# Modulation products in float32r parts, gate products ranked behind the main stream, one modulation vector moved

## The chip, the cores and the metric

The kernel runs on one core of a Trainium2 chip. The metric is device time in microseconds (us) for one launch, the median of several runs. TensorE (PE) multiplies; VectorE (DVE), ScalarE (ACT) and GpSimd (POOL) work on tiles; SyncE (SP) issues the DMA transfers.

## The reference

One inference step of a two-layer diffusion backbone for 128 context and 512 latent tokens, all in float32, outputs included. In each layer:

```python
sh1, sc1, g1, sh2, sc2, g2 = split(silu(c) @ w_mod + b_mod, 6)      # "modulation vectors" 0..5
h = rmsnorm(x, g_pre_mix) * (1 + sc1) + sh1
qa, ka, va, qbd, kvbd, kbr, qc, kc, vc, gates = split(h @ w_in)
oa, ob, oc = mixer A (windowed), mixer B (multi-head latent), mixer C (rotary)   # attention, 8 heads each
m = sum over A, B, C of sigmoid(gate) * (o @ w_o);  mixed = m @ w_out
x = x + g1 * rmsnorm(mixed, g_post_mix)
h = rmsnorm(x, g_pre_mlp) * (1 + sc2) + sh2
x = x + g2 * rmsnorm(square(relu(h @ w_mlp1)) @ w_mlp2, g_post_mlp)
```

The modulation uses one conditioning vector for the latent tokens and another for the context tokens.

## The kernel before

Tokens are five tiles of 128, features eight chunks of 128. A float32 product is made of three float32r products: each operand is split into a high part (ACT copies it to float32r: `wh`, `hh`) and a low part (DVE subtracts: `wl`, `hl`), and `mm3` adds high x high, high x low and low x high in PSUM. Weights come as 128x1024 pieces (`unit`): one DMA into `wr`, then the two splits.

The start (`first_norm`): the five token tiles `x` are normalised and transposed (`xn`, `nps`, `hf`). In the meantime modulation vectors 1 and 0 of layer 0 are computed, in two halves of 512 columns: eight transfers of 1 MB (`mw`) bring the weights, and plain float32 matmuls (`lps<-mw,scT`, 32 of them, 2x512 out) multiply them with the two conditioning vectors `scT`. A row of sums (`modrow`) is copied out by ACT, transposed (`modt`) and added to the bias (`modT`, `gsT`); with these `hf` is scaled and shifted and split into `hh` and `hl`. Then mixer B's projection begins: 288 columns (`sps<-wh,hh`, its weights split ahead of the second half's modulation), in a first round over chunks 0 to 3 of all five token tiles and a second over chunks 4 to 7, and then 384 columns.

The gates (`gate_gen`, L1573): 24 pieces of 128 columns per layer, each in two halves of 24 matmuls (`gps`), a tanh (`th`) and a store. They are the work with which other stages are filled: `drive` steps through a main generator and adds credit at a rate to the streams beside it; at credit 1 a stream records one step (one gate half, or one `w_mod` piece). In mixer B the gates' rate is `GATE_RATE_B` for seven heads and 1 in the last; in A and C it is `GATE_RATE`; what is left at the end of C is recorded at once, and four halves go into the merge. The other filler is `mod_gen`: the remaining modulation vectors, on DVE (`macc`: 14 of 16 steps are a multiply-add on 128x512), ten steps per vector. Before the change each layer computes vectors 2, 3, 4 beside A and C, and layer 0's MLP computes vector 5 and layer 1's 0 and 1.

What is recorded is then put in order by a planner (`Recorder.schedule`): a list scheduler with a cost for each operation (`cost`) chooses for each engine, at the time that it models, the ready operation of the lowest rank. On TensorE the rank is the place in the record, less `high_priority`'s offset; on the others it is the latest time from the pass before. The instructions are emitted in that order, all from one line, L528, and each engine works through its own in order. In mixer B the PSUM banks are two pairs (`big`) and a ring of four, shared by `tps` (transposed probabilities), `ops` (their products with the values), `pjps`, `qrps` and `gps`.

Of the kernel before, what the change touches and what calls it, by code (L numbers as in the profile page):

```python
# [11 lines left out]
F32 = mybir.dt.float32  # L12
# [5 lines left out]
P = 128  # L18
D = 1024
KC = 8  # L20
# [11 lines left out]

GATE_RATE = ((0.3, 0.3, 0.235, 0.241), (0.213, 0.3, 0.195, 0.156))
PROJ_RATE = ((0.26, 0.583, 0.277), (0.326, 0.93, 0.22))
GATE_RATE_B = 0.03
MOD_RATE = 0.3
MOD_RATE_B = 0.0
GATES_LAST = 4
GATES_FIRST = 2
LAG = 2  # L40
# [7 lines left out]
KEPT = 4  # L48
ACT_BUFS = 10
UP_RATE = (0.5, 0.5)  # L50
DOWN_RATE = (1.0, 0.5)

# [115 lines left out]
class Recorder:  # L168
# [23 lines left out]
    def cost(self, op, outs, ins):  # L192

        n = outs[0].idx.size if outs else 1
        e, name = op.eng, op.name
        if op.dma:
            return 0.4, 0.4
        if e == "tensor":
            passes = 4 if name == "matmul" and ins[-1].dt == F32 else 1
            t = max(0.108, n * passes / 2400 + 0.013)  # L200
            return t, t + 0.17
        src = max([v.idx.size for v in ins] or [n])
        if e == "vector":
            if name == "scalar_tensor_tensor":
                t = 0.21 + 1.04e-3 * src
            elif name in ("tensor_scalar", "tensor_copy"):
                t = 0.16 + (1.04e-3 if any(v.root.space == "PSUM" for v in ins) else 0.54e-3) * src
            else:
                t = 0.15 + 1.04e-3 * src
            return t - 0.08, t  # L210
        if e == "scalar":
            t = 0.19 + 0.83e-3 * src
            if any(isinstance(op.kw.get(k), View) for k in ("bias", "scale")):
                t += 0.09
            if "accum_out" in op.kw:
                t += 0.1
            return t - 0.1, t
        if name == "tensor_scalar":
            t = 0.3 + 0.8e-3 * src
        elif op.kw.get("op") == ALU.pow or ALU.pow in op.args:  # L220
            t = 0.4 + 0.16 * src
        else:
            t = 0.15 + 2.25e-3 * src
        return t, t


    def record(self, eng, name, args, kw):
# [12 lines left out]
            v = op.views[0]  # L240
            op.wait = (v.hi - v.lo) * v.idx.size * 4
        op.time = op.busy, op.wait
        op.both = eng == "gpsimd" and name == "tensor_tensor" and outs[0].idx.size > 4
        for views, write in ((ins, False), (outs, True)):
            for v in views:
                r, m, keep, seen = v.root, v.mask(), [], False
# [139 lines left out]
    def one(self, everything, look):  # L386
# [3 lines left out]
        now = {e: [] for e in engines}  # L390
        order, self.done, self.given = [], [], []
        count = 0
        pool_end, net, half = 0.0, 0.0, 0.0

        def less(s, t, todo):
            nonlocal count
# [39 lines left out]
        while True:  # L436
# [32 lines left out]
            if o.dma:  # L469
                net = max(net, t + 1.6) + wait / 370e3  # L470
                wait = net + 0.7 - t
            elif e == "vector" and o.sb and pool_end > t:
                more = 0.62 * min(pool_end - t, busy / 0.38)
                busy, wait = busy + more, wait + more
            elif o.both:
                busy, wait = 1.2 * busy, 1.2 * wait
                pool_end = t + busy
            elif e == "tensor":
                if t - free[e] > 2.6:
                    half = t + (6.8 if t - free[e] > 4 else 3.4)  # L480
                if t < half:
                    busy, wait = 2 * busy, wait + busy
# [49 lines left out]
class Step:  # L532
# [70 lines left out]
    def setup(self, ctx):  # L603
# [34 lines left out]
        self.gkc = c.tile([P, 64], F32, name="gkc")  # L638
        self.sink = c.tile([P, 8], F32, name="sink")
        self.scT = c.tile([P, 2, 8], F32, name="scT")  # L640
        self.modT = [c.tile([P, 6, 8, 2], F32, name=f"modT{l}") for l in range(DEPTH)]
        self.vecT = [c.tile([P, 64], F32, name=f"vecT{l}") for l in range(DEPTH)]
        self.gsT = [c.tile([P, 2, 8, 2], F32, name=f"gsT{l}") for l in range(DEPTH)]
# [21 lines left out]
    def cond(self):  # L665

        nc, I = self.nc, self.I
        cT = self.sm.tile([P, 16], F32, name="cT")
        self.small_rows_T(cT, [I["c"].rearrange("o (a b) -> (o a) b", b=P), I["c_ctx"].rearrange("(a b) -> a b", b=P)])
        e = self.sm.tile([P, 16], F32, name="ce")  # L670
        nc.scalar.activation(e, cT, AF.Exp, scale=-1.0)
        nc.vector.tensor_scalar(e, e, 1.0, None, ALU.add)
        r = self.sm.tile([P, 16], F32, name="cr")
        nc.vector.reciprocal(r, e)
        nc.vector.tensor_tensor(self.scT.rearrange("p s k -> p (s k)"), cT, r, ALU.mult)
        for l in range(DEPTH):
# [146 lines left out]
    def first_norm(self, pool, xin):  # L823
# [17 lines left out]
        mod, gs = self.modT[0], self.gsT[0]  # L841
        w = I["w_mod"][0]
        for n in range(2):
            if n == 1:
                self.first = self.proj_units(I["w_in"][0], 768 + 384, 288, 3)
            for v in (1, 0):
                ps = self.lin_ps()
                for kh in range(2):
                    raw = pool.tile([P, 4, 512], F32, name="mw", tag="mw", bufs=8)
                    nc.sync.dma_start(raw, self.wsrc(w, 4 * kh, 4, v * D + n * 512, 512))  # L850
                    for i in range(4):
                        k = 4 * kh + i
                        nc.tensor.matmul(ps[:2, :], self.scT[:, :, k], raw[:, i], start=k == 0, stop=k == KC - 1)
                row = pool.tile([2, 512], F32, name="modrow", tag="modrow", bufs=2)
                nc.scalar.activation(row, ps[:2, :], AF.Copy)
                tps = self.bank("modt", "pt")
                pv = tps[:, :8].rearrange("p (n s) -> p n s", s=2)
                for j in range(4):
                    nc.tensor.transpose(pv[:, j, :], row[:, j * P:j * P + P], self.ident[:2, :2])
                ks = slice(4 * n, 4 * n + 4)  # L860
                nc.vector.tensor_tensor(mod[:, v, ks], pv, self.vecT[0][:, 8 * v:8 * v + 8][:, ks].unsqueeze(2).to_broadcast([P, 4, 2]), ALU.add)
                if v:
                    self.gains(0, 0, ks)
            for k in range(4 * n, 4 * n + 4):
# [5 lines left out]
                        nc.vector.tensor_scalar(hf[:, k, c], hf[:, k, c], g, b, ALU.mult, ALU.add)  # L870
                nc.scalar.activation(self.hh[:, k, :], hf[:, k, :], AF.Copy)
                nc.vector.tensor_tensor(self.hl[:, k, :], hf[:, k, :], self.hh[:, k, :].bitcast(F32), ALU.subtract)


    def proj_units(self, w, c0, n, kn):
# [700 lines left out]
    def gate_gen(self, pool, l):  # L1576
# [3 lines left out]
        for n in range(24):  # L1580
            wh, wl = self.unit(self.wsrc(w, 0, 8, 2208 + n * P, P), (8, P))
            for hf in range(2):
                c = slice(hf * NH, hf * NH + NH)
                ps = self.bank("gps", self.gtag)
                for k in range(KC):
                    self.mm3(ps[:, :NH], wh[:, k, :], wl[:, k, :], self.hh[:, k, c], self.hl[:, k, c], k == 0, k == KC - 1)
                th = pool.tile([P, NH], F32, name="th", tag="th", bufs=2)
                nc.scalar.activation(th, ps[:, :NH], AF.Tanh, scale=0.5)
                nc.sync.dma_start(self.th_d[l][n][:, c], th)
# [323 lines left out]
    def run(self):  # L1913
        nc, tc, I, O = self.nc, self.tc, self.I, self.O
        with ExitStack() as ctx:
# [23 lines left out]
            for l in range(DEPTH):  # L1939
                self.fine = False  # L1940
                stack2 = ExitStack()
                fpool = stack2.enter_context(pool(f"fill{l}", sides[1 - l % 2]))
                mods = [self.mod_gen(fpool, l, (2, 3, 4))]
                gates_left = self.gate_gen(fpool, l)
                gl = [itertools.islice(gates_left, 48 - GATES_LAST)]
                fills = gl + mods
# [98 lines left out]
                with pool(f"up{l}", side) as mp:  # L2045
# [4 lines left out]
                    modp = fstack.enter_context(pool(f"md{l}", hside))  # L2050
                    mods = [self.mod_gen(modp, l, (5,), 2)]
                    if not last:
                        mods = [itertools.chain(*mods, self.mod_gen(modp, l + 1, (0, 1), 2))]
                    kept = {"pool": kstack.enter_context(pool(f"kept{l}", hside))}
                    halfs = self.halfs()

# [99 lines left out]
```

## Time and profile before

| | us |
|---|---|
| median of 3 runs (2334.31 to 2335.96) | 2334.68 |
| the profiled execution | 2327.95 |
| its span, first to last instruction | 2326.2 |
| PE busy | 2277.6 |
| DVE busy | 1705.0 |
| ACT busy | 1204.0 |

The profile comes from one execution, which took less than the median of the runs shown. A matmul's busy time reaches past the point at which the next can start, so idle time of PE is larger than the listed one.

### The profile page before, as it was taken

What the parts mean: (1) busy time and instruction counts of PE and PEld (TensorE: products, weight loads), DVE (VectorE), ACT (ScalarE), POOL (GpSimd) and SP (SyncE); (2) the same over time, 40 slices, a digit from 0 to 9 for tenths busy, and PEclk for the clock granted to TensorE, in tenths of its full rate; (3) what the DMA queues carried; (4) which work ended last, traced back from release to release, by engine and by line L of the source; (5) the groups of instructions that cost most, each with busy time, mean ns of one, the idle gap of its engine ahead of it and who ended that gap; (6) DMA issues with size and microseconds to landing.
All of it is one profiled execution on the core that took longest, in us unless ns stands there. A gap on an engine that the chain in (4) does not pass through costs nothing. (4 is left out here: it accounts for less than half of the span.)

```text
span 2326.2 us, 39127 instructions
## 1 busy us (share of the span) xinstructions
PE 2277.6 (98%) x14303; PEld 2086.7 (90%) x14303; DVE 1705.0 (73%) x3707; ACT 1204.0 (52%) x2860; POOL 260.8 (11%) x315
## 2 busy tenths in 40 slices
PE   8999999999999999999999999999999999999998
PEld 4988999999998999888889889999899999998886
DVE  3688598997675998767377867999947569895445
ACT  5477455566435555632265764656643356554222
POOL 1023022222001000000021211222210000000000
PEclk9999999999999999999999999999999999999999
DMA  7431334333663454755244222434346545536332
GB/s 258 117 84 53 88 111 137 106 109 97 225 207 113 151 184 144 241 190 165 68 136 116 65 79 80 138 101 123 110 145 205 172 136 177 166 127 208 121 118 82
DMA packets 252448, 317.08 MB, mean 136 GB/s; under 512 B 37328, under 2 KB 169696, under 8 KB 251744
## 3 DMA queue, kind: packets, MB, share of 16 engines
q1 hardware_dynamic: 252256, 314.58, 43.6%
q8 instruction: 113, 1.85, 0.3%
q14 instruction: 79, 0.65, 0.1%
HBM read 251.84 MB, written 57.44 MB: 133 GB/s over the span
## 5 line engine op out<-in xcount | busy, mean ns | idle before, releaser
L528 ACT ACTIVATE wh<-wr 128x256 fp32r<-128x256 f32 (+5 forms) x772 | 273.7, 420 | 306.2 <-PE lps L528 166.5
L528 DVE TENSOR_TENSOR wl<-wr,wh 128x256 fp32r<-128x256 f32 (+5 forms) x772 | 303.4, 441 | 147.9 <-ACT wh L528 143.0
L528 PE MATMUL lps<-wh,ah 128*128 128x512 f32 x640 | 253.0, 395 | 0.0
L528 PE MATMUL lps<-wh,al 128*128 128x512 f32 x640 | 252.4, 394 | 0.0
L528 PE MATMUL lps<-wl,ah 128*128 128x512 f32 x640 | 251.6, 393 | 0.0
L528 POOL TENSOR_SCALAR pt<-pt,rc 128x640 f32<-128x640 f32 (+1 forms) x192 | 174.1, 915 | 629.4 <-DVE rc L528 523.2
L528 POOL TENSOR_TENSOR rs<-ss,mhalf 128x1 f32<-128x1 f32 x60 | 39.1, 652 | 1302.7 <-DVE ss L528 1302.7
L528 DVE TENSOR_TENSOR pl<-tps,ph 128x512 fp32r<-128x512 f32 (+2 forms) x240 | 147.9, 630 | 31.1 <-ACT ph L528 28.4
L528 ACT ACTIVATE pt<-sps,nm 128x640 f32<-128x640 f32 (+2 forms) x192 | 141.7, 741 | 42.1 <-DVE nm L528 36.3
L528 ACT ACTIVATE ph<-tps 128x512 fp32r<-128x512 f32 (+2 forms) x240 | 130.2, 556 | 35.4 <-PE tps L528 33.1
L528 PEld LDWEIGHTS lps<-wl,ah 128*128 128x128 f32 x640 | 120.1, 188 | 28.6 <-issue 0.5
L528 PEld LDWEIGHTS lps<-wh,ah 128*128 128x128 f32 x640 | 120.2, 188 | 27.8 <-issue 0.5
L528 PEld LDWEIGHTS lps<-wh,al 128*128 128x128 f32 x640 | 120.1, 188 | 27.6
L528 PE MATMUL sps<-h2h,wh 128*128 128x320 f32 (+2 forms) x464 | 144.3, 311 | 0.0
L528 PE MATMUL tps<-ident,pt 128*128 128x128 f32 x896 | 140.5, 275 | 3.6 <-POOL pt L528 2.9
L528 PE MATMUL sps<-h2l,wh 128*128 128x320 f32 (+2 forms) x464 | 143.1, 308 | 0.0
L528 PE MATMUL sps<-h2h,wl 128*128 128x320 f32 (+2 forms) x464 | 143.1, 308 | 0.0
L528 DVE SCALAR_TENSOR_TENSOR macc<-wr,scT,macc 128x512 f32<-128x512 f32 x168 | 126.4, 786 | 6.0 <-DMA wr<-in_w_mod 5.7
L528 PE MATMUL gps<-hh,wh 128*128 128x320 f32 x384 | 120.0, 312 | 2.7 <-ACT th L528 1.8
L528 PE MATMUL gps<-h2h,wh 128*128 128x320 f32 x384 | 119.7, 312 | 0.2 <-DVE pl L528 0.2
L528 PEld LDWEIGHTS tps<-ident,pt 128*128 128x128 f32 x896 | 106.7, 141 | 14.5 <-POOL pt L528 5.5
L528 PE MATMUL sps<-ol,wh 128*128 128x320 f32 x384 | 118.6, 309 | 0.5 <-DVE ol L528 0.5
(329 smaller groups left out, 6785.2 us busy)
## 6 DMA issues: line engine op xcount, KB each, us to landing
wr<-in_w_in SPq DMA_DIRECT2D x72, 512.0 KB, 4.0
wr<-in_w_mlp SPq DMA_DIRECT2D x72, 512.0 KB, 4.0
wq<-in_w_mlp SPq DMA_DIRECT2D x56, 512.0 KB, 4.0
wr<-in_w_mod SPq DMA_DIRECT2D x48, 512.0 KB, 3.8
ar<-a SPq DMA_DIRECT2D x56, 320.0 KB, 3.8
mr<-in_w_mod SPq DMA_DIRECT2D x32, 512.0 KB, 5.9
th<-th SPq DMA_DIRECT2D x96, 160.0 KB, 2.0
tg<-th SPq DMA_DIRECT2D x48, 320.0 KB, 3.5
```

The lines of the kernel that those rows point to most:

```text
L528: getattr(getattr(self.nc, o.eng), o.name)(*args, **kw)
```

## The change

The 32 float32 products of the start become 64 float32r ones: ACT and DVE split each 128x512 block of `w_mod` into `wh` and `wl`, the conditioning vectors are split once (`scs`: two high columns, two low ones), and each block is multiplied with all four columns, so that the row of sums has four rows, added in pairs behind the transposes. The split of mixer B's first weights is recorded behind both halves instead of between them. Gate matmuls are recorded with an offset of 200 places to the rear, and the gates' rate beside mixer B is 0.1 in place of 0.03. Vector 2 of layer 1 is computed in layer 0's MLP, in place of beside layer 1's mixers. The planner's costs of some operations are changed.

```diff
-GATE_RATE_B = 0.03
+GATE_RATE_B = 0.1
+GATES_BEHIND = 200
-DOWN_RATE = (1.0, 0.5)
+DOWN_RATE = (1.3, 0.5)
...
         if e == "tensor":
-            passes = 4 if name == "matmul" and ins[-1].dt == F32 else 1
-            t = max(0.108, n * passes / 2400 + 0.013)
+            if ins[-1].dt == F32:
+                t = n * 4 / 2400 + 0.013 if name == "matmul" else 0.108
+                t = max(0.18, t) if name == "matmul" else t
+            else:
+                t = n / 2400 + (0.018 if n > 400 else 0.013) if n > 128 else 0.085
...
             if "accum_out" in op.kw:
-                t += 0.1
+                return t, t
...
-        op.both = eng == "gpsimd" and name == "tensor_tensor" and outs[0].idx.size > 4
+        op.both = eng == "gpsimd" and name in ("tensor_tensor", "tensor_scalar") and outs[0].idx.size > 4
...
-                more = 0.62 * min(pool_end - t, busy / 0.38)
+                more = pool_hold * min(pool_end - t, busy / (1 - pool_hold))
...
+        for i in range(2):
+            nc.vector.tensor_copy(self.scs[:, :, i], self.scT[:, i, :])
+            nc.vector.tensor_tensor(self.scs[:, :, 2 + i], self.scT[:, i, :], self.scs[:, :, i].bitcast(F32), ALU.subtract)
...
-            if n == 1:
-                self.first = self.proj_units(I["w_in"][0], 768 + 384, 288, 3)
...
-                        nc.tensor.matmul(ps[:2, :], self.scT[:, :, k], raw[:, i], start=k == 0, stop=k == KC - 1)
...
+                        nc.scalar.activation(wh, raw[:, i], AF.Copy)
+                        nc.vector.tensor_tensor(wl, raw[:, i], wh.bitcast(F32), ALU.subtract)
+                        nc.tensor.matmul(ps[:4, :], self.scs[:, k, :], wh, start=k == 0, stop=False)
+                        nc.tensor.matmul(ps[:4, :], self.scs[:, k, :], wl, start=False, stop=k == KC - 1)
...
+                nc.vector.tensor_tensor(mod[:, v, ks], pv[:, :, 2:4], mod[:, v, ks], ALU.add)
...
+        self.first = self.proj_units(I["w_in"][0], 768 + 384, 288, 3)
...
-                for k in range(KC):
-                    self.mm3(ps[:, :NH], wh[:, k, :], wl[:, k, :], self.hh[:, k, c], self.hl[:, k, c], k == 0, k == KC - 1)
+                with self.tc.high_priority(offset=-GATES_BEHIND):
+                    for k in range(KC):
+                        self.mm3(ps[:, :NH], wh[:, k, :], wl[:, k, :], self.hh[:, k, c], self.hl[:, k, c], k == 0, k == KC - 1)
...
-                mods = [self.mod_gen(fpool, l, (2, 3, 4))]
+                mods = [self.mod_gen(fpool, l, (2, 3, 4) if l == 0 else (3, 4))]
...
-                        mods = [itertools.chain(*mods, self.mod_gen(modp, l + 1, (0, 1), 2))]
+                        mods = [itertools.chain(*mods, self.mod_gen(modp, l + 1, (0, 1, 2), 2))]
```

ScalarE at the start, before: the fifth token tile's normalisation to the first chunk scaled with the first half's modulation (`x_126` is the context tile, `hf_168` the transposed tokens, `modrow` the row of sums).

```order
L528 ACTIVATE xn,ss<-x_126 128x1024
L528 ACTIVATE hf_168<-nps 128x4x128 x2
L528 ACTIVATE modrow<-lps 2x512
L528 ACTIVATE hf_168<-nps 128x4x128 x2
L528 ACTIVATE modrow<-lps 2x512
L528 ACTIVATE hf_168<-hf_168,modT_281,gsT_283 128x512
L528 ACTIVATE hh<-hf_168 128x640
```

The same stretch of ScalarE now, from the first row of sums on (`wh<-mw` is the high part of a block of `w_mod`, `wh<-wr` that of mixer B's first weights).

```order
L533 ACTIVATE modrow<-lps 4x512
L533 ACTIVATE wh<-mw 128x512 x8
L533 ACTIVATE hf_173<-nps 128x4x128
L533 ACTIVATE modrow<-lps 4x512
L533 ACTIVATE wh<-mw 128x512 x9
L533 ACTIVATE modrow<-lps 4x512
L533 ACTIVATE wh<-mw 128x512 x4
L533 ACTIVATE wh<-wr 128x432
L533 ACTIVATE hf_173<-hf_173,modT_375,gsT_384 128x512
L533 ACTIVATE hf_173<-hf_173,modT_375,gsT_384 128x128
L533 ACTIVATE hh<-hf_173 128x640 x2
```

All 32 blocks of `w_mod` are split ahead of the first scaled chunk, and mixer B's first weights behind them; VectorE has its 32 `wl<-mw` in the same places.

TensorE in mixer B of layer 0, second pair of heads, before: the last scores and transposes ahead of the keys' projection (`sps<-ckh,wh`), which takes its PSUM pair over from `qd`, the queries.

```order
L528 MATMUL sps<-krT,qrT 128x320
L528 MATMUL tps<-ident,pt 128x128 x4
L528 MATMUL qrps<-identr,qrst 128x128 x4
L528 MATMUL ops<-ph,Vb 128x512
L528 MATMUL sps<-ckh,wh 128x384
L528 MATMUL sps<-ckl,wh 128x384
L528 MATMUL sps<-ckh,wl 128x384
```

The same place now (`gps` are gate products).

```order
L533 MATMUL sps<-krT,qrT 128x320
L533 MATMUL tps<-ident,pt 128x128
L533 MATMUL gps<-hl,wh 128x320
L533 MATMUL tps<-ident,pt 128x128
L533 MATMUL gps<-hh,wl 128x320
L533 MATMUL tps<-ident,pt 128x128
L533 MATMUL gps<-hh,wh 128x320
L533 MATMUL tps<-ident,pt 128x128
L533 MATMUL gps<-hl,wh 128x320
L533 MATMUL gps<-hh,wl 128x320
L533 MATMUL gps<-hh,wh 128x320
L533 MATMUL gps<-hl,wh 128x320
L533 MATMUL sps<-ckh,wh 128x384
```

Seven gate products now stand between the last scores and the keys' projection, one or a few at a time. Counted in TensorE's order from the first query product of mixer B (`sps<-qlh`) to the first key transposed for A (`kps`), gate products rise from 212 to 380 in layer 0 and from 216 to 384 in layer 1. From there to the last product of C's values they fall from 720 to 552 and from 580 to 552. Between the end of C and the first product of the merge, where nothing else is left, they fall from 48 to 34 in layer 0 and from 188 to 34 in layer 1. Places where TensorE changes between a gate product and another rise from 204 to 1132.

## Rows read from the trace of the kernel before

**Rows 1.** The page's first lines: span, and busy time of each engine.
```profile
span 2326.2 us, 39127 instructions
PE 2277.6 (98%) x14303; PEld 2086.7 (90%) x14303; DVE 1705.0 (73%) x3707; ACT 1204.0 (52%) x2860; POOL 260.8 (11%) x315
```

**Rows 2.** Busy time by stretch: bounds, length, engines (x instructions), granted clock, DMA.
```profile
core 0: us, PE busy (x) PEld busy (x) DVE busy (x) ACT busy (x) POOL busy (x), PEclk, DMA share, GB/s
0.00:45.20 45.20, 37.36 (x119) 12.04 (x119) 14.35 (x48) 22.41 (x41) 9.04 (x16) 1.00 0.89 308
112.00:225.00 113.00, 107.83 (x724) 97.85 (x722) 91.47 (x191) 84.09 (x195) 28.74 (x38) 1.00 0.27 70
225.00:259.00 34.00, 33.32 (x232) 32.52 (x232) 13.45 (x35) 13.82 (x39) 1.74 (x3) 1.00 0.36 110
...
950.00:1181.00 231.00, 231.00 (x1044) 189.54 (x1043) 146.30 (x279) 82.66 (x195) 6.94 (x9) 1.00 0.52 168
1254.00:1366.00 112.00, 107.03 (x718) 97.48 (x717) 93.73 (x194) 84.32 (x196) 28.22 (x37) 1.00 0.30 78
1430.00:1712.00 282.00, 274.94 (x1972) 258.34 (x1971) 255.91 (x624) 173.81 (x451) 71.84 (x79) 1.00 0.38 110
```

**Rows 3.** The same view for gate products alone (tile gps), mixer B, layer 0.
```profile
112.00:225.00 113.00, 7.34 (x47) 6.63 (x45) 0.87 (x2) 1.00 0.27 70
225.00:259.00 34.00, 25.98 (x168) 25.05 (x168) 3.07 (x7) 1.00 0.36 110
```

**Rows 4.** TensorE in order of time, mixer B: start, us, matmul.
```profile
138.84 0.50 PE L528 MATMUL ops<-ph,Vb 128*128 128x512 f32 x1
140.02 0.41 PE L528 MATMUL sps<-ckh,wh 128*128 128x384 f32 x1 [0.68 <-DVE qd L528]
```

**Rows 5.** Groups of 0 to 62 us: busy, mean ns, idle before.
```profile
L528 PE MATMUL lps<-mw,scT 128*2 128x512 f32 x64 | 29.1, 601 | 0.0
...
L528 DVE TENSOR_TENSOR hl<-hf,hh 128x640 fp32r<-128x640 f32 x8 | 6.2, 822 | 2.4 <-ACT hh L528 2.3
...
L528 ACT ACTIVATE hh<-hf 128x640 fp32r<-128x640 f32 x8 | 5.4, 723 | 0.0
...
L528 ACT ACTIVATE hf<-hf,modT,gsT 128x512 f32<-128x512 f32 x4 | 3.1, 808 | 2.8 <-DVE modT L528 2.8
```

**Rows 6.** TensorE in order of time: mixer B's first products of 288 and 384 columns.
```profile
45.23 0.40 PE L528 MATMUL sps<-wh,hh 128*128 128x288 f32 x1
...
63.12 0.39 PE L528 MATMUL lps<-wh,hh 128*128 128x384 f32 x1
```

**Rows 7.** VectorE in order of time: the low parts of chunks 4 to 7.
```profile
49.95 3.03 DVE L528 TENSOR_TENSOR hl<-hf,hh 128x640 fp32r<-128x640 f32 x4 [1.44 <-ACT hh L528]
```

**Rows 8.** DMA rate in 40 equal slices of 0 to 45.2 us.
```profile
GB/s 0 29 297 421 243 3 60 359 406 433 417 390 388 401 393 392 384 392 384 384 391 386 382 393 384 386 386 390 384 380 391 390 240 148 40 75 283 117 360 253
```

**Rows 9.** Groups of the whole span, shapes apart: busy, mean ns, idle before.
```profile
L528 DVE TENSOR_TENSOR pl<-tps,ph 128x512 fp32r<-128x512 f32 x176 | 118.0, 685 | 29.0 <-ACT ph L528 26.5
...
L528 DVE SCALAR_TENSOR_TENSOR macc<-mr,scT,macc 128x512 f32<-128x512 f32 x112 | 78.6, 744 | 5.3 <-DMA mr<-in_w_mod 5.0 <-ACT macc L528 0.2
...
L528 DVE TENSOR_TENSOR wl<-wr,wh 128x512 fp32r<-128x512 f32 x28 | 18.8, 682 | 3.0 <-ACT wh L528 2.7
...
L528 ACT ACTIVATE wh<-wr 128x512 fp32r<-128x512 f32 x28 | 16.1, 627 | 9.3 <-DMA wr<-in_w_in 9.1
```

**Rows 10.** TensorE in order of time: transposes of the first and the third token tile.
```profile
7.75 3.83 PE L528 MATMUL nps<-ident,xn 128*128 128x128 f32 x16
...
15.70 1.09 PE L528 MATMUL nps<-ident,xn 128*128 128x128 f32 x8 [0.94 <-POOL xn L528]
```

**Rows 11.** Busy time by stretch for tile macc alone, layer 1's A and C.
```profile
1430.00:1712.00 282.00, 11.22 (x72) 8.92 (x72) 61.56 (x83) 3.60 (x5) 1.00 0.38 110
```

More of the change, by code (lines that the diff above doesn't have):

```diff
@@ L392, in one @@
         count = 0
-        pool_end, net, half = 0.0, 0.0, 0.0
+        pool_end, pool_hold, net, half = 0.0, 0.0, 0.0, 0.0
         def less(s, t, todo):
@@ L477, in one @@
                 pool_end = t + busy
+                pool_hold = 0.62 if o.name == "tensor_tensor" else 0.3
             elif e == "tensor":
@@ L640, in setup @@
         self.scT = c.tile([P, 2, 8], F32, name="scT")
+        self.scs = c.tile([P, 8, 4], F32R, name="scs")
         self.modT = [c.tile([P, 6, 8, 2], F32, name=f"modT{l}") for l in range(DEPTH)]
@@ L852, in first_norm @@
                         k = 4 * kh + i
-                        nc.tensor.matmul(ps[:2, :], self.scT[:, :, k], raw[:, i], start=k == 0, stop=k == KC - 1)
-                row = pool.tile([2, 512], F32, name="modrow", tag="modrow", bufs=2)
-                nc.scalar.activation(row, ps[:2, :], AF.Copy)
+                        if i % 2 == 0:
+                            hi = self.ws.tile([P, 1024], F32R, name="wh", tag="wh", bufs=self.NW)
+                            lw = self.ws.tile([P, 1024], F32R, name="wl", tag="wl", bufs=self.NW)
+                        wh, wl = (t[:, i % 2 * 512:i % 2 * 512 + 512] for t in (hi, lw))
+                        nc.scalar.activation(wh, raw[:, i], AF.Copy)
+                        nc.vector.tensor_tensor(wl, raw[:, i], wh.bitcast(F32), ALU.subtract)
+                        nc.tensor.matmul(ps[:4, :], self.scs[:, k, :], wh, start=k == 0, stop=False)
+                        nc.tensor.matmul(ps[:4, :], self.scs[:, k, :], wl, start=False, stop=k == KC - 1)
+                row = pool.tile([4, 512], F32, name="modrow", tag="modrow", bufs=2)
+                nc.scalar.activation(row, ps[:4, :], AF.Copy)
                 tps = self.bank("modt", "pt")
-                pv = tps[:, :8].rearrange("p (n s) -> p n s", s=2)
+                pv = tps[:, :16].rearrange("p (n s) -> p n s", s=4)
                 for j in range(4):
-                    nc.tensor.transpose(pv[:, j, :], row[:, j * P:j * P + P], self.ident[:2, :2])
+                    nc.tensor.transpose(pv[:, j, :], row[:, j * P:j * P + P], self.ident[:4, :4])
                 ks = slice(4 * n, 4 * n + 4)
-                nc.vector.tensor_tensor(mod[:, v, ks], pv, self.vecT[0][:, 8 * v:8 * v + 8][:, ks].unsqueeze(2).to_broadcast([P, 4, 2]), ALU.add)
+                nc.vector.tensor_tensor(mod[:, v, ks], pv[:, :, 0:2], self.vecT[0][:, 8 * v:8 * v + 8][:, ks].unsqueeze(2).to_broadcast([P, 4, 2]), ALU.add)
+                nc.vector.tensor_tensor(mod[:, v, ks], pv[:, :, 2:4], mod[:, v, ks], ALU.add)
                 if v:
```

## The prediction

> **What bounds the kernel now.** I read the page first: PE is busy 2277.6 of 2326.2 us [rows 1], so anything that doesn't shorten PE's own work, or its waits, moves nothing. Then the busy time by stretch. The reader is to see two kinds of stretch there. In the MLP PE is busy 231.00 of 231.00 us [rows 2]; nothing can be won but work. In mixer B's first seven heads it is idle 113.00 - 107.83 = 5.2 us in layer 0 and 112.00 - 107.03 = 5.0 in layer 1, in A and C of layer 1 282.00 - 274.94 = 7.1 [rows 2]. The listed idle time is too small: in the timeline a product begins at 138.84 and the next at 140.02, 1.18 us apart, and only 0.68 of it counts as idle, since a matmul's busy time runs past the point where the next could start [rows 4]. Adding, over the 724 matmuls of mixer B's stretch, what each start-to-start distance has above the usual one of its form gives some 13 us (an estimate), the same in layer 1, and 22 in layer 1's A and C. Gate products could stand in these holes, but the view for gate products shows 47 of them in the 113 us of seven heads, and 168 in the 34 us of the last [rows 3], where PE idles only 0.7 us [rows 2].
>
> **The change, part by part.**
>
> *The start.* PE loses 64 records (two for each of 32 products) that fill 29.1 us [rows 5] and gets 64 float32r products of the same columns; at half a record's time each pair costs what one record did, so about 14.5 us go. That is not the gain, since they stood in front of mixer B's first product at 45.23 [rows 6] without a pause, and the new ones wait for ACT and DVE. What ends last now? The transfers run at 380 to 400 GB/s until about 36 us [rows 8]; behind the last `w_mod` block come mixer B's first weights, 128 x 8 x 288 x 4 bytes = 1.18 MB, 3 us, so `w_mod` is there at about 33. Its last four blocks cost one ACT split (0.63) and four DVE splits (0.68 each) [rows 9]: 36.4, or 37 with the small instructions in between. One megabyte takes 2.7 us to come and 4 x 0.68 = 2.7 on DVE, so DVE just keeps pace. Mixer B's first product can start at about 38, 7 us earlier. But all scaling is now queued behind the splits on ACT: 8 `hh` (5.4), 4 wide scalings (3.1) [rows 5] and 13 smaller ones (four narrow scalings, a row of sums, eight weight halves) of at most 0.63: 14 to 17 us behind 35.6, so the last `hh` is done at 50 to 52 and its `hl` at 51 to 53. Before it was done at 49.95 + 3.03 = 52.98 [rows 7]. So the last chunk comes hardly earlier; what PE gains is that from 38 to 52 it works off the first round and most of the second. The stage of 288 columns took 63.12 - 45.23 = 17.9 us [rows 6]. Only chunk 7's products, 15 of 120, must wait for the end: 52 + 2 us plus transposes, 55 to 56, against 63.12. I take 6 us of these 7 or 8, since the fourth piece of the 384-column weights now waits for a `wr` buffer that is split late. Bounds: 8 us (17.9 us without a pause from 37.3), and nothing (PE works tile by tile, so that each tile waits for chunk 7, 52.98 + 10).
>
> *More gates beside mixer B.* The order puts 168 more gate matmuls there in each layer. The work is the same in sum; what counts is which holes it fills. They are taken from A and C (168 fewer in layer 0, 28 in layer 1) and from the lump behind C in layer 1, which falls from 188 to 34: there PE has nothing to fill. Where the keys' projection waited for `qd` (0.68 listed), seven gate products now stand ahead of it. Three such waits, the scores' and the transposes' are the bulk of the 13 us. From both ends: all of it filled, 13 us per layer; nothing filled, since the planner's times are not the chip's and a hole is often not where a gate stands, 0; less than nothing is the slower rival below. I take a third, 4.5 us per layer, 9 in both: nearer to the listed 5 us than to 13.
>
> *A and C.* Layer 1 loses vector 2. All `macc` work there takes DVE 61.56 us [rows 11], a third of it is 20.5; DVE falls from 255.9 of 282 us (91%) to about 235 (83%). PE's waits there are for `pl`, `pt` and others behind a full DVE. Layer 0 has fewer fillers. I take 2 us in layer 1 and nothing in layer 0; bounds 8 won (a third of 22), 4 lost.
>
> *The vector in the MLP.* 28 multiply-adds of 0.744 us [rows 9] add 21 us to DVE's 146.30 of 231 us [rows 2], 72% with the few others; PE stays busy throughout, and the DMA share is 0.52 [rows 2]. Nothing, if a `wl` is late 1 us. SP's queue gets eight more `mr` loads between the weight loads, with room.
>
> *More changes of tile on PE* (204 to 1132): a group of four transposes with gate products between costs a few ns more for each; I take 1 us of loss.
>
> *The planner's costs* have no duration of their own; they are in the order.
>
> Sum: -6 - 9 - 2 + 1 = -16 us. The profiled execution took 2327.95 us, 6.7 less than the median shown; carried over, 2327.95 becomes 2312 and the median 2334.68 becomes 2318.7. I forecast 2319.
>
> **The rivals.**
>
> *Only the start gains.* A list scheduler's gap is a fraction of a microsecond, and 0.68 us here and there [rows 4] may move rather than go. For: nothing fills a hole that the planner misplaces. Against: PE works in order, and a gate ahead of a late product costs nothing. -6 - 1 = -7: 2328.
>
> *The start gains nothing*, the rest does: PE works tile by tile, or the clock is low when mixer B begins. The first token tile's transposes take 3.83 / 16 = 0.24 us each, the third's 1.09 / 8 = 0.14 [rows 10]: PE began at the lower of its two levels (1.2 and 2.4 GHz) and rose after some work. Now it has 14.5 us of products spread from 13 to 37, with pauses, in place of a closed row. If it falls back, the first 7 us of products take 7 more: 2334.7 - 16 + 7 = 2326. The Trainium skill ("TensorE: Matmul & The Clock Gate", Part 1) says that the throttled clock is the default and that activity releases it; by that rule pauses speak against this change, while the rows show that a mixture of short transposes and pauses was enough to raise it.
>
> *Slower: the gates hold a bank.* A gate half of 24 products that is spread over single gaps keeps one of the ring's four PSUM banks for some 13 us (200 products over 113 us) instead of 24 x 25.98 / 168 = 3.7 [rows 3], while transposes, value products and their evacuations share three. For it: a bank of transposes is held for `ph` and `pl`, and `pl` alone takes 0.685 us [rows 9]; PE does a part in about that. Against: the order was made with the ring in view. There are 5 such parts in 8 heads and 2 layers, 80: at half a `pl`, 0.35 us each, 28 us are lost in place of 9 won: 2334.7 - 6 - 2 + 1 + 28 = 2356. It decides from 7 / 80 = 0.09 us per part on; at 0.2 us the time is 2344.
>
> *It doesn't do what it says:* start and holes both unchanged, 2334 to 2335.
>
> **How the numbers follow.** Chances: forecast 0.50 (own range 2309 to 2326), only the start 0.20, start without gain 0.10, bank 0.13, no effect 0.07. A measurement of this kernel can tell about 0.2%, 4.7 us, from no change: below 2330.0 is faster, above 2339.4 slower. Faster: nearly all of the first three cases less a margin, 0.76; same: the remainder and the last case, 0.11; slower 0.13. The range for 8 in 10 reaches from 2306 (all bounds half used: 8, 16 and 5 us won) to 2335, which holds the second, third and last case and leaves the bank's out.
>
> **What would show it.** In the changed profile: mixer B's first product at 37 to 40 and the first of 384 columns at 54 to 58; the last `hl` of chunk 7 at 51 to 53; PE's listed idle time in mixer B's seven heads below 4 us with some 200 gate products there; DVE below 240 us in layer 1's A and C; the MLP of layer 0 still without idle time. The forecast is wrong if PE waits for `tps` or `ops` banks more often than before, if the 384 columns begin after 60, or if A and C, with fewer gates, idle by more than mixer B saves.

## The result and the profile after

The changed kernel takes 2311.14 us (median of 4 runs, 2311.10 to 2311.33), the kernel before 2334.49 us (4 runs, 2333.51 to 2335.96): a ratio of 0.990, 95% interval 0.988 to 0.992, faster by 23.4 us. The forecast was 2319, within 2306 to 2335. The profiled executions are 16.8 us apart (2327.95 and 2311.13); of them -16 had been forecast. The sum was right, but not for the reasons given, as the experiments show: some terms were too high, one that was put at nothing was large, and that they cancel is luck.

The first lines of the page after, beside [rows 1]:

```profile
span 2309.3 us, 39145 instructions
PE 2266.9 (98%) x14303; PEld 2090.8 (91%) x14303; DVE 1727.6 (75%) x3731; ACT 1221.2 (53%) x2876; POOL 260.1 (11%) x315
```

Busy time by stretch, after, in the bounds of [rows 2] (length, engines with their instructions, granted clock, DMA share, GB/s). The stages now begin some 5 us earlier in layer 0 and 7 us earlier in layer 1, so that the same bounds hold nearly, but not quite, the same work. The last row is layer 0's MLP up to its end:

```profile
0.00:45.20 45.20, 33.46 (x157) 16.71 (x157) 31.68 (x76) 38.11 (x73) 9.26 (x16) 0.96 0.83 291
112.00:225.00 113.00, 109.98 (x756) 103.92 (x756) 87.90 (x179) 79.93 (x185) 27.75 (x35) 1.00 0.31 79
1254.00:1366.00 112.00, 109.82 (x756) 103.50 (x754) 87.11 (x177) 79.85 (x186) 28.68 (x35) 1.00 0.30 79
1430.00:1712.00 282.00, 278.54 (x2040) 267.35 (x2039) 242.39 (x612) 177.73 (x458) 72.46 (x79) 0.99 0.30 87
950.00:1181.00 231.00, 229.86 (x1044) 187.87 (x1043) 166.95 (x314) 82.76 (x196) 8.61 (x10) 1.00 0.59 189
...
950.00:1176.21 226.21, 226.21 (x1018) 184.75 (x1017) 162.60 (x305) 78.35 (x185) 7.12 (x9) 1.00 0.59 188
```

TensorE's listed idle time in mixer B falls from 5.2 and 5.0 us to 113.00 - 109.98 = 3.0 and 2.2, in layer 1's A and C from 7.1 to 3.5. In the MLP's second half there is none, as before: the 1.1 us in the row that ends at 1181 lie behind the MLP's end at 1176.21, in layer 1's first projection. Gate products in the same stretches, beside [rows 3]: 163 in place of 47.

```profile
112.00:225.00 113.00, 33.02 (x163) 26.40 (x163) 2.65 (x6) 1.00 0.31 79
225.00:259.00 34.00, 25.99 (x149) 23.05 (x149) 2.63 (x7) 1.00 0.30 95
```

The keys' projection of [rows 4] still waits for `qd`, behind its gates: 0.83 us from start to start in place of 1.18 (TensorE in order of time, after).

```profile
131.15 0.31 PE L533 MATMUL gps<-hl,wh 128*128 128x320 f32 x1
131.98 0.41 PE L533 MATMUL sps<-ckh,wh 128*128 128x384 f32 x1 [0.52 <-DVE qd L533]
```

The start: mixer B's first product, the first of 384 columns (both TensorE; before in [rows 6]), and VectorE's last `hl` (before in [rows 7]):

```profile
39.46 0.40 PE L533 MATMUL lps<-wl,scs 128*4 128x512 f32 x1 [0.69 <-DVE wl L533]
39.84 0.53 PE L533 MATMUL sps<-wh,hh 128*128 128x288 f32 x2
...
58.46 0.33 PE L533 MATMUL lps<-wh,hh 128*128 128x384 f32 x1
```

```profile
50.94 0.83 DVE L533 TENSOR_TENSOR hl<-hf,hh 128x640 fp32r<-128x640 f32 x1
```

Where the time went, from the first product of each stage in both profiles (us from the span's start):

| until the first product of | before | after | stage, after less before |
|---|---|---|---|
| layer 0: mixer B's heads | 112.17 | 106.69 | -5.5 |
| the merge (B, A, C and the lump of gates) | 593.85 | 582.87 | -5.5 |
| the MLP | 688.05 | 679.66 | +2.6 |
| layer 1: mixer B's projection | 1181.18 | 1176.21 | +3.4 |
| mixer B's heads | 1253.78 | 1246.83 | -2.0 |
| the merge | 1739.35 | 1716.66 | -15.7 |
| the MLP | 1830.98 | 1812.54 | +4.2 |
| the last product with `ah` (the second half of layer 1's MLP) | 2317.03 | 2300.31 | +1.7 |

Layer 1 is the first surprise: its mixers gain 15.7 us, of which 3.4 are the eight `mps` products of vector 2, now in layer 0's MLP. Some of the gain comes back in the merge, where by the order 14 more gate products stand (2 us) and 0.7 us of idle time are listed (95.88 us less 95.17 busy) where there was none.

### The profile page after: what moved, and what is told of

Same layout as the page of the kernel before. It is cut to its first block, busy times and chain, and to the rows that moved or that the text cites. A ratio compares the mean times of both kernels' runs of the same rounds, so it can differ in the third digit from the quotient of the medians.

```text
span 2309.3 us, 39145 instructions
## 1 busy us (share of the span) xinstructions
PE 2266.9 (98%) x14303; PEld 2090.8 (91%) x14303; DVE 1727.6 (75%) x3731; ACT 1221.2 (53%) x2876; POOL 260.1 (11%) x315
## 3 DMA queue, kind: packets, MB, share of 16 engines
q8 instruction: 113, 1.85, 0.3%
## 4 chain that ended last, share of the span: by engine, by line
PE 85%; DVE 7%; ACT 3%; DMA 3%; issue 1%; SPq 0%; POOL 0%; DVEq 0%; POOLq 0%; ACTq 0%
PE sps L533 30%; PE lps L533 28%; PE gps L533 11%; PE fps L533 5%; PE ops L533 4%; PE tps L533 3%; DMA orw<-o 2%; PE mps L533 1%; DVE wl L533 1%; DVE macc L533 1%; PE pjps L533 1%; PE nps L533 1%; DVE pl L533 1%; DMA wr<-in_w_in 1%; ACT wh L533 1%
## 5 line engine op out<-in xcount | busy, mean ns | idle before, releaser
L533 ACT ACTIVATE wh<-wr 128x256 fp32r<-128x256 f32 (+4 forms) x756 | 274.1, 425 | 303.7 <-PE lps L533 165.2
L533 DVE TENSOR_TENSOR wl<-wr,wh 128x256 fp32r<-128x256 f32 (+4 forms) x756 | 304.6, 448 | 145.7 <-ACT wh L533 141.3
L533 POOL TENSOR_SCALAR pt<-pt,rc 128x640 f32<-128x640 f32 (+2 forms) x192 | 173.0, 908 | 622.7 <-DVE rc L533 493.2
L533 PE MATMUL gps<-hl,wh 128*128 128x320 f32 x384 | 120.5, 314 | 0.0
L533 PE MATMUL gps<-hh,wl 128*128 128x320 f32 x384 | 120.4, 313 | 0.0
L533 PE MATMUL gps<-h2l,wh 128*128 128x320 f32 x384 | 120.1, 313 | 0.0
```

The lines of the kernel that those rows point to most:

```text
L533: getattr(getattr(self.nc, o.eng), o.name)(*args, **kw)
```

## The experiments

Theory: the single parts add up as forecast (start 6, gates beside mixer B 9, the vector 2, the rest nothing). Rivals: only the start gains, or the gain comes from something that had no term, such as the planner's costs. Each kernel was timed in five rounds with the kernel before, in three batches on three chips, in which that had medians of 2332.28, 2333.30 and 2331.97 us. The changed kernel was not timed again in them, so a difference of 1 to 3 us from its 2311.14 is told from noise only where the interval of its ratio lies clear of 0.988 to 0.992.

**The start alone.** The kernel before with the lines of the change in `first_norm`:

```diff
+        self.scs = c.tile([P, 8, 4], F32R, name="scs")
...
-                        nc.tensor.matmul(ps[:2, :], self.scT[:, :, k], raw[:, i], start=k == 0, stop=k == KC - 1)
+                        nc.tensor.matmul(ps[:4, :], self.scs[:, k, :], wh, start=k == 0, stop=False)
+                        nc.tensor.matmul(ps[:4, :], self.scs[:, k, :], wl, start=False, stop=k == KC - 1)
```

> The kernel before with the float32r parts of the first modulation products alone (gates, vectors and planner's costs as before). Theory (what PE gains at the start stays, 4.7 us at the first product of 384 columns): 2329.5, between 2327 and 2332, and that product at 58 to 59.5 us. Rival (the start's gain is given back in mixer B, which is bound by other engines): 2333 to 2336, with the first gate at 82 but mixer B's end at the same time as before.

2335.41 us (2332.57 to 2336.38), ratio 1.0013 (1.0004 to 1.0022): no gain, but a loss of 3.1 us. The first product of 288 columns comes at 39.97, but that of 384 at 62.17. The trace says why. SyncE's queue, VectorE and TensorE of this kernel:

```profile
41.93 8.85 SPq L528 DMA_DIRECT2D wr<-in_w_in  x3
...
51.81 0.43 SPq L528 DMA_DIRECT2D gkva<-in_g_kva  x1
```

```profile
57.40 0.48 DVE L528 SCALAR_TENSOR_TENSOR zb<-zb,rs,gkva 128x256 f32<-128x256 f32 x1 [2.70 <-DMA gkva<-in_g_kva]
```

```profile
58.03 0.41 PE L528 MATMUL bps<-ident,zb 128*128 128x128 f32 x2 [2.38 <-DVE zb L528]
```

Three weight loads stand 8.85 us in SyncE's queue for a free `wr`, whose splits are late behind the 64 new ones; behind them stands the load of 256 small values, VectorE waits 2.70 us for it and TensorE 2.38 us for VectorE. In the changed kernel, whose order comes from the new costs, that load is issued at 49.31 and nothing waits for it.

**The late load on another queue.** The kernel of the first experiment with one edit:

```diff
-        nc.sync.dma_start(gkva, I["g_kva"][l:l + 1, :].to_broadcast([P, 256]))
+        (nc.sync if l else nc.gpsimd).dma_start(gkva, I["g_kva"][l:l + 1, :].to_broadcast([P, 256]))
```

> The first experiment's kernel (before with the new start alone) with one load moved: the 256 values gkva of layer 0 are loaded by GpSimd's queue in place of SyncE's, where they stood behind three weight loads that waited 8.85 us for a free buffer. There VectorE stood 2.70 us for gkva at 57.40 and TensorE 2.38 us behind it. Theory (that queue ate the start's gain): the wait goes, the first product of 384 columns comes at 59 to 60 in place of 62.17, the first of mixer B's heads at about 108.5 in place of 111.01, and the time is 2332 to 2334 against 2335.4. Rival (the weights of 384 columns hold it as well): 62.2 and 2335.4 unchanged.

2333.20 us (2327.89 to 2336.14), ratio 1.0004 (0.9994 to 1.0014). The load is issued early, the wait is gone, and the 384 columns begin 2.5 us sooner (GpSimd, then TensorE):

```profile
20.73 0.76 POOL L528 DMA_DIRECT2D gkva<-in_g_kva  x1 [1.44 <-DVE wl L528]
```

```profile
59.68 0.39 PE L528 MATMUL lps<-wh,hh 128*128 128x384 f32 x1
```

Mixer B's heads begin at 108.50, 3.7 us before those of the kernel before, as the theory had it; and still the kernel is no faster. So something later takes the start's gain back; what the next two experiments find is a part of it.

**The change without its start.**

```diff
-        self.scs = c.tile([P, 8, 4], F32R, name="scs")
...
+                        nc.tensor.matmul(ps[:2, :], self.scT[:, :, k], raw[:, i], start=k == 0, stop=k == KC - 1)
```

> The changed kernel with the plain float32 products of the start put back (all else as changed). Theory (the parts add up): 5 us above the changed kernel, 2316, between 2314 and 2319. Rival (the gates beside mixer B gain only since the start is early): 2322 or more.

2312.69 us (2311.08 to 2313.21), ratio 0.9914 (0.9901 to 0.9928), below both forecasts: by the medians the start is worth 1.6 us in the end, by the intervals it isn't told from nothing, though the heads begin 4.7 us earlier with it (106.69 against 111.35). Part of the loss is spread over the whole kernel. In the last stage, where TensorE never waits, the same products take 2301.84 - 2077.11 = 224.73 us without the start, 225.50 with it, and 224.73 in the kernel of the next experiment (first and last product with `ah`; without the start, with it, next experiment):

```profile
2077.11 0.39 PE L533 MATMUL lps<-wh,ah 128*128 128x512 f32 x1
...
2301.84 0.39 PE L533 MATMUL lps<-wl,ah 128*128 128x512 f32 x1
```

```profile
2074.81 0.39 PE L533 MATMUL lps<-wh,ah 128*128 128x512 f32 x1
...
2300.31 0.40 PE L533 MATMUL lps<-wl,ah 128*128 128x512 f32 x1
```

```profile
2073.60 0.39 PE L533 MATMUL lps<-wh,ah 128*128 128x512 f32 x1
...
2298.33 0.39 PE L533 MATMUL lps<-wl,ah 128*128 128x512 f32 x1
```

**Where the operands lie.** The new tile `scs` takes 128 bytes per partition among the constants, and all that is laid out behind it moves by as much. The changed kernel with 512 bytes in its place; TensorE's order is the same row for row:

```diff
-        self.scs = c.tile([P, 8, 4], F32R, name="scs")
+        self.scs = c.tile([P, 128], F32R, name="scs")[:, :32].rearrange("p (k s) -> p k s", s=4)
```

> The changed kernel with the tile scs (4 x 8 values, 128 bytes per partition) laid out in 512 bytes, so that every tile behind it moves by another 384 bytes; nothing else. In every kernel with the new start layer 1's MLP products of 256 columns come 117.8 ns apart and those of 384 columns 177.9, in every kernel without it 113.4 and 175.0, and the last stage is 1.7 us longer. Theory (it is where the operands lie in memory): 113.4 and 175.0 come back, layer 1's MLP takes 486.1 us in place of 487.8, all together 2308 to 2310. Rival (it has another cause, such as the higher number of instructions ahead): unchanged, 2311.

2309.80 us (2309.16 to 2310.64), ratio 0.9902 (0.9886 to 0.9917): 1.3 less than the changed kernel by the medians, not told from it by the interval. The last stage is back at 224.73 us. In layer 0's MLP both sizes are back at what they take without the start (256 columns 118.3 ns from start to start, 119.9 in the changed kernel; 384 columns 175.4 and 178.4). In layer 1's MLP the 384 columns come back by half (177.9 in the changed kernel, 176.4 here, 175.0 without the start; means over all 96 products) and the 256 columns not at all (117.8). Compared product by product over the whole kernel (mean start-to-start distances of like products, waits and slow stretches left out, an estimate), the changed kernel loses 2.1 us against this one and 2.6 us against the one without the start. So the place of the operands does set a small part of a product's time, and 128 more bytes took back about half of what the start gave. In the version with these 512 bytes and the old gates' rate (the next to last experiment) both sizes come back wholly in both layers, 113.4 and 175.0 in layer 1, where the old rate alone has 117.8 and 177.9. Which address matters stays open; that it is an address, and not the number of instructions ahead, is borne out twice.

**The gates alone.** The kernel before, old costs, with the gates' two numbers:

```diff
-GATE_RATE_B = 0.03
+GATE_RATE_B = 0.1
+GATES_BEHIND = 200
...
+                with self.tc.high_priority(offset=-GATES_BEHIND):
```

> The kernel before with the gates' rank 200 places back and their rate beside mixer B 0.1, all else as before, the planner's costs too. Theory (gate products in mixer B's holes are the main gain, 6 us per layer, less some 4 for changes of tile and for A and C): 2326, between 2322 and 2329. Rival (the planner's new costs are what puts gates where the holes are): 2331 to 2336.

2319.32 us (2318.38 to 2319.78), ratio 0.9943 (0.9930 to 0.9955), 13.0 us faster: the largest part, and more than expected. The two numbers were then taken back one at a time from the changed kernel.

**The gates' old rank.**

```diff
-GATES_BEHIND = 200
+GATES_BEHIND = 0
```

> The changed kernel with GATES_BEHIND = 0, so that gates have their own rank again; GATE_RATE_B stays 0.1. As many gate products stand beside mixer B as in the changed kernel (380 and 384), but in lumps: TensorE changes between a gate and another product 228 times in place of 1132. Theory (what fills holes is that single gates stand between others, not how many there are in the stage): TensorE's waits in mixer B go back to about 14 us per layer from 9.0 and 7.7, those of layer 1's A and C to about 22 from 17: 5 + 6 + 5 lost less some 6 us of slower tile changes given back, 2311 + 10 = 2321 (2317 to 2327). Rival (the number beside mixer B is what counts): 2309 to 2314.

2318.61 us (2316.29 to 2319.26), ratio 0.9936 (0.9923 to 0.9948): 7.5 us are lost by the medians, with the same number of gates beside mixer B, and the interval lies clear of the changed kernel's.

**The gates' old rate.**

```diff
-GATE_RATE_B = 0.1
+GATE_RATE_B = 0.03
```

> The changed kernel with GATE_RATE_B = 0.03: 212 and 216 gate products beside mixer B as in the kernel before, 177 in the lump behind layer 1's C, but spread singly (1014 tile changes). Theory (spreading counts, the number little): 2311 to 2316, with mixer B's waits at about 11 us per layer. Rival (the number beside mixer B counts): mixer B's waits at 14 us per layer, 2318 to 2323.

2310.54 us (2309.77 to 2313.95), ratio 0.9906 (0.9893 to 0.9920): as fast as the changed kernel. How many gates stand beside mixer B is worth nothing; that they stand singly is what counts. But mixer B's waits are as long as before (11.5 us of listed idle time in both layers, in the table below), so the reason that I had expected (they would fall to 11 us per layer from 14) is wrong too: the time comes from A and C. Busy time from the first key of A to the last value product of C, layer 0, then layer 1, first of the changed kernel, then with the old rate, then with the old rank:

```profile
273.07:576.66 303.59, 297.38 (x2191) 282.42 (x2189) 277.45 (x700) 186.06 (x489) 72.99 (x79) 1.00 0.36 106
1412.58:1709.65 297.07, 294.84 (x2181) 283.82 (x2182) 251.40 (x649) 185.18 (x485) 72.46 (x79) 0.99 0.29 84
```

```profile
254.43:573.54 319.11, 317.42 (x2348) 305.68 (x2347) 280.20 (x709) 192.13 (x503) 72.93 (x79) 1.00 0.37 109
...
1391.80:1688.86 297.06, 295.66 (x2201) 286.17 (x2199) 249.96 (x649) 184.69 (x483) 69.48 (x79) 0.99 0.30 87
1688.86:1715.08 26.22, 26.22 (x181) 26.18 (x180) 7.61 (x19) 9.79 (x26) 0.00 (x0) 1.00 0.51 168
```

```profile
275.31:585.63 310.32, 300.50 (x2190) 284.94 (x2190) 278.03 (x701) 185.56 (x490) 72.58 (x79) 0.99 0.35 103
...
1420.47:1717.95 297.48, 293.67 (x2181) 281.92 (x2181) 252.82 (x653) 184.69 (x488) 70.17 (x79) 1.00 0.30 86
```

With the old rate TensorE's listed idle time there is 319.11 - 317.42 = 1.7 us in layer 0, against 6.2 in the changed kernel and 9.8 with the old rank. It can even afford the lump of 181 products behind C (the row 1688.86), in which nothing is filled. The same reading of every kernel, both layers added (length less TensorE's busy time; mixer B is up to the first key of A, A and C up to C's last value product, in layer 1 with the lump behind it):

| kernel | gates beside B, per layer | tile changes | idle in B | idle in A and C | median us |
|---|---|---|---|---|---|
| before | 212, 216 | 204 | 11.5 | 13.9 | 2331.97 to 2334.49 |
| costs alone | 212, 216 | 210 | 12.4 | 8.6 | 2324.42 |
| gates alone | 380, 384 | 1142 | 5.0 | 12.7 | 2319.32 |
| old rank | 380, 384 | 228 | 8.1 | 15.0 | 2318.61 |
| old costs | 380, 384 | 1142 | 5.0 | 12.7 | 2318.64 |
| old rate | 212, 216 | 1014 | 11.5 | 3.1 | 2310.54 |
| changed | 380, 384 | 1132 | 5.9 | 9.9 | 2311.14 |

The listed idle time understates the waits [rows 4], and the medians hold the clock as well (below), so that the differences of the two need not agree. The gates are one stock of fillers. What mixer B gets of them A and C lack: from the old rate to the changed kernel 5.6 us of idle time go in B and 6.8 come in A and C.

**The vector back in layer 1.**

```diff
-DOWN_RATE = (1.3, 0.5)
+DOWN_RATE = (1.0, 0.5)
...
-                mods = [self.mod_gen(fpool, l, (2, 3, 4) if l == 0 else (3, 4))]
+                mods = [self.mod_gen(fpool, l, (2, 3, 4))]
...
-                        mods = [itertools.chain(*mods, self.mod_gen(modp, l + 1, (0, 1, 2), 2))]
+                        mods = [itertools.chain(*mods, self.mod_gen(modp, l + 1, (0, 1), 2))]
```

> The changed kernel with vector 2 of layer 1 back in its mixers (DOWN_RATE 1.0 as before), the rest as changed. Theory (the vector in the MLP frees VectorE in layer 1's A and C): the MLP's second half in layer 0 takes 231 us in place of 234.05, of which 3.4 us are TensorE products that go back into layer 1's mixers, A and C of layer 1 wait some 5 us more for a busier VectorE: 2311 + 5 = 2316 (2313 to 2318). Rival (A and C gained from the spread gates alone, and VectorE had room): 2309 to 2312.

2311.30 us (2309.64 to 2313.28), ratio 0.9907 (0.9894 to 0.9921): the move is worth nothing, as the rival had it. Layer 1's A and C, in the stretch of [rows 2] and of the table above:

```profile
1430.00:1712.00 282.00, 278.26 (x2024) 264.67 (x2023) 261.48 (x646) 178.61 (x459) 69.28 (x79) 1.00 0.37 108
```

VectorE is busy 261.48 of 282 us, more than before (255.91), and TensorE 278.26, all but as much as in the changed kernel (278.54, VectorE 242.39). A VectorE at 93% isn't what TensorE waited for.

**The planner's costs.** Taken out of the changed kernel, and put alone into the kernel before (the same cost lines in the two directions, shown as they were put in; `pool_hold`, which stayed in when they were taken out, makes no difference without the line on `op.both`):

```diff
-            passes = 4 if name == "matmul" and ins[-1].dt == F32 else 1
-            t = max(0.108, n * passes / 2400 + 0.013)
+            if ins[-1].dt == F32:
...
-                t += 0.1
+                return t, t
...
-        op.both = eng == "gpsimd" and name == "tensor_tensor" and outs[0].idx.size > 4
+        op.both = eng == "gpsimd" and name in ("tensor_tensor", "tensor_scalar") and outs[0].idx.size > 4
```

> The changed kernel with the planner's costs of before. Theory (the costs matter little): 2311 to 2315. Rival (the costs carry the gain): 2319 or more.

2318.64 us (2317.02 to 2319.95), ratio 0.9941 (0.9929 to 0.9954): 7.5 us slower than the changed kernel by the medians, with the interval clear of its own: 0.4 us short of the rival's 2319.

> The kernel before with the planner's new costs and nothing else. Taken out of the changed kernel they cost 7.5 us. Theory (they are a better order by themselves, in A and C above all): 2325 to 2328, with layer 0's and layer 1's stages from the first key of A to the last value product of C some 2 to 3 us shorter each. Rival (they were worth something only with the single gates, whose products the old costs put at the wrong length): 2331 to 2335 as the kernel before.

2324.42 us (2322.03 to 2326.33), ratio 0.9970 (0.9959 to 0.9981): 7.6 us. A and C of both layers become shorter, by 1.8 and 4.2 us; their idle time falls from 13.9 to 8.6 us, mixer B's doesn't (the table). With the old costs in the changed kernel it is the same stage that loses, 12.7 us in place of 9.9. A and C, layer 0 and layer 1, of the kernel before and then with the new costs alone:

```profile
258.78:586.47 327.69, 320.99 (x2360) 307.04 (x2359) 282.94 (x712) 192.40 (x508) 76.00 (x79) 1.00 0.37 106
1401.05:1711.55 310.50, 303.26 (x2220) 286.56 (x2219) 274.90 (x691) 187.25 (x490) 71.84 (x79) 1.00 0.36 105
```

```profile
262.02:587.90 325.88, 321.75 (x2360) 308.65 (x2358) 283.13 (x712) 192.41 (x508) 73.73 (x79) 0.99 0.37 107
1403.14:1709.46 306.32, 301.85 (x2221) 288.00 (x2219) 274.88 (x691) 187.09 (x490) 72.39 (x79) 0.99 0.37 107
```

The costs are a part of their own, and the forecast had no term for it.

**Two versions more.** The changed kernel with 512 bytes for `scs` and another rate, and in the second another rank too:

```diff
-GATE_RATE_B = 0.1
+GATE_RATE_B = 0.03
```

> The changed kernel with scs laid out in 512 bytes and GATE_RATE_B = 0.03 together. Alone they gave 2309.8 and 2310.5 against 2311.1. If the two add up, 2309 (2308 to 2310.5); if the order's chance details decide by more than that, anywhere from 2308 to 2313.

2306.26 us (2305.12 to 2310.37), ratio 0.9895 (0.9878 to 0.9912): the lowest median, about 5 us below the changed kernel's and 3 below the expected sum, but the interval overlaps the changed kernel's (0.988 to 0.992), so it isn't shown to be faster.

```diff
-GATE_RATE_B = 0.1
-GATES_BEHIND = 200
+GATE_RATE_B = 0.06
+GATES_BEHIND = 100
```

> The changed kernel with scs in 512 bytes, GATE_RATE_B = 0.06 (260 and 264 gate products beside mixer B) and GATES_BEHIND = 100, which spreads them still more singly (1384 tile changes in place of 1132). Theory (the gates are one stock of fillers, and what one stage has of them another lacks): no better than the others, 2308 to 2312, since more changes of tile cost 1 to 2 us and mixer B's waits lie between 8 and 14 us. Rival (a place between is better than either): below 2307.

2312.15 us (2311.22 to 2312.32), ratio 0.9917 (0.9904 to 0.9929): no better than the changed kernel, as expected.

## Why the prediction was right in its sum and wrong in its parts

*The start, -6.* At mixer B's heads it is -5.5 us: right, and its steps with it (39.84 for "37 to 40", last `hl` at 51.8 for "51 to 53", 58.46 just behind "54 to 58"). As a term of the sum it is -1.6 by the medians, not told from nothing. Two things failed: "I take 6 us" took a gain at one place for a gain at the end, and of the queue the prediction followed only the weights that wait for a late `wr`, not the small load behind them (in the order of the old costs it eats 2.5 us). The rival that the start gains nothing named the wrong cause: TensorE's clock did fall back once behind its pauses, as feared, but at 25.94 TensorE waits for a split block of `w_mod` again, so that the fall cost little or nothing. (The prediction saw a "mixture of short transposes and pauses" before the clock rose; it left out six long modulation products, 3.24 us from 11.52 on, between the two groups of [rows 10].) The changed kernel's row of that stretch, and that wait:

```profile
17.90:21.30 3.40, 3.40 (x16) 2.46 (x14) 1.58 (x3) 2.97 (x7) 1.65 (x2) 0.50 1.05 387
```

```profile
25.94 0.39 PE L533 MATMUL lps<-wl,scs 128*4 128x512 f32 x1 [0.16 <-DVE wl L533]
```

*Gates beside mixer B, -4.5 per layer.* The step "what counts is which holes it fills" was right, "more gates beside mixer B" as the cause was wrong. Mixer B's waits did fall (listed idle time of both layers from 11.5 to 5.9 us), but the number of gates there is worth nothing in the sum (old rate: 2310.54); the single placing by rank is worth 7.5 us by the medians, wherever it is. Of the rival that the gates hold a bank, the list of TensorE's waits in layer 0's mixer B shows one case at most: `lps` behind a gate's `th`, 0.6 us.

*A and C, -2 in layer 1 for a freer VectorE.* Wrong cause: VectorE fell to 242 ("below 240"), and with it at 261 the time is the same. The waits there fell for the gates' rank and the planner's costs (layer 1's listed idle time there, lump included: 7.2 us before, 5.2 with the old rank, 5.5 with the old costs, 4.7 with the vector back, 3.6 in the changed kernel). In layer 0, idle time stayed (6.7 before, 6.2 after), as "nothing" had it.

*The vector in the MLP, 0.* Right, also that the MLP stays without idle time. It costs 3.4 us there, the moved products, of which layer 1's mixers are rid.

*Changes of tile, +1.* Not shown: no run has the changes of tile without the filled holes, and the term stays open.

*The planner's costs, "in the order".* This is the step that failed: they were counted at nothing since they have no duration, and are worth 7.5 us (taken out of the changed kernel; 7.6 put alone into the one before), in A and C above all.

*"Carried over, ... the median 2334.68 becomes 2318.7."* The profiled execution of before was taken as standing 6.7 us below its median for good. It was a run with a high mean granted clock (0.998; 1 is TensorE at its upper level, 2.4 GHz, throughout). Over 42 runs of the kernel before beside the experiments:

| mean granted clock of the run | 0.994 | 0.995 | 0.996 | 0.997 | 0.998 |
|---|---|---|---|---|---|
| runs | 5 | 8 | 15 | 11 | 3 |
| mean time, us | 2335.1 | 2333.7 | 2332.2 | 2330.5 | 2327.1 |

The changed kernel had 0.998 in all four runs. At that clock the two are 2327.1 - 2311.2 = 15.9 us apart, and the other 7.5 us of the 23.4 go with a clock that falls less often: the clocks of the four runs with the median 2334.49 are not on record, but by the table such a time belongs to 0.994 to 0.995. Before's profile shows one such fall. TensorE in order of time, then the stretch behind by busy time:

```profile
1199.93 0.34 PE L528 MATMUL lps<-wh,h2l 128*128 128x384 f32 x1
1201.98 0.40 PE L528 MATMUL lps<-wh,h2h 128*128 128x288 f32 x1 [1.71 <-DVE h2h L528]
```

```profile
1203.80:1207.20 3.40, 3.40 (x16) 3.40 (x15) 3.30 (x23) 2.03 (x7) 1.11 (x2) 0.50 0.00 0
1207.20:1220.00 12.80, 12.80 (x82) 12.50 (x81) 8.59 (x32) 7.66 (x25) 3.07 (x5) 1.00 0.56 125
```

TensorE waits 2.05 us from start to start, and soon after runs 3.40 us at 0.50 of its clock (1.2 in place of 2.4 GHz), which costs half of that, 1.7 us. That such falls come from the waits is read from their places, not tried by itself: the fourteen profiles of this study show 29 of them between the start and the last stage's end; 18 begin within 4 us behind one of TensorE's longest 129 waits, and of the 24 longest of these (1.85 to 2.70 us from start to start) 11 are followed by one. If the two had nothing to do with each other, less than one of the 29 would lie there (an estimate: 129 times 4 us of 14 times 2250). Of the eleven other falls nine begin within 4.4 us of the first of sixteen `mps` products of one column each, one of the changed kernel's among them, while its waits of 2.05 us at 1194.70 and 1.91 us at 1709.65 are followed by none:

```profile
1452.87 1.95 PE L533 MATMUL mps<-ones,macc 128*128 128x1 f32 x16 [0.67 <-ACT pz L533]
```

```profile
1454.90:1458.30 3.40, 3.40 (x16) 3.10 (x15) 2.73 (x13) 2.26 (x5) 0.00 (x0) 0.50 0.00 0
```

The Trainium skill ("TensorE: Matmul & The Clock Gate", Part 1) says that the gate looks at how busy TensorE has been; the rows agree, in that 27 of the 29 falls come behind a wait or behind such narrow products. So a wait taken away may be worth more than its length; no run shows that by itself.

What is left: the parts alone, by medians, are -7.6 (costs), -13.0 (gates), +3.1 (start) and 0 (vector, taken out of the changed kernel), together -17.5, against -23.4 measured. Some 5 us of the difference is the start by the medians, which costs 3.1 with the old order and brings 1.6 with the new one. A part of all these figures is the clock: set against the runs of the kernel before that had the same granted clock (the table), the parts are about -6 (costs), -8 (gates) and +2 (start), together -12, against -15.9 (estimates). The 4 us between stay open.

## What to carry to other kernels

Where a planner sets the order, its costs are an edit like any other: time them alone. Fillers for a busy engine are one stock; give them the lowest rank so that they stand singly in every stage, rather than move them to one. A gain at the start of a kernel is counted at its end, and two profiled executions are compared at the same granted clock.

## What the runs showed of the hardware

A tile of 128 bytes among the constants changed the time of products that don't touch it: 384 columns from 175.0 to 177.9 ns, 256 columns from 113.4 to 117.8 (layer 1's MLP, start to start), 0.8 us in a stage of 225 us without a wait. And runs of one kernel whose mean granted clock was 0.994 took 8 us longer than those with 0.998. In kernels whose TensorE is listed as busy 98% of the time the clock fell to 0.50, mostly for 3.4 us, behind some single waits of 1.2 to 2.7 us and behind some groups of products one column wide.
